# Loading the first 2 KiB of the first tile's runs from ScalarE's queue, beside the other 62 KiB from SP's

## Chip, cores, metric

One core of a Trainium2 chip. The metric is the device time of one execution in microseconds. A kernel's time is the median of its runs. A ratio is the mean time of one kernel's fast runs over that of the other's of the same rounds on the same chip, so it is not quite the ratio of the medians quoted; the brackets after it hold its 95% interval.

## The reference

```python
# x: (1024, 4096) float32, axis = -1
mean = np.mean(x, axis=axis, keepdims=True)
return ((x - mean) ** 2).astype(np.float32)
```

## The kernel before

Two tiles, each of 512 rows: 128 partitions with four rows of 4096 numbers each, so one contiguous run of 64 KiB for each partition. Both tiles stay in SBUF from the start; nothing waits for a buffer. The first load is cut: a small transfer of 2 KiB runs, then the other 62 KiB of each run.

```python
HEAD = 512
H = D * 9 // 16
...
for i in range(ntiles):                       # ntiles = 2
    x_tile = io.tile([P, Q * D], F32)         # Q = 4, D = 4096
    cuts = [0, HEAD, Q * D] if i == 0 else [0, Q * D]
    for lo, hi in zip(cuts, cuts[1:]):
        nc.sync.dma_start(out=x_tile[:, lo:hi], in_=x_t[i][:, lo:hi])
...
for i in range(ntiles):
    row = [tiles[i][:, q * D:(q + 1) * D] for q in range(Q)]
    m3 = mean_on_act(row[3])                  # ScalarE
    m0 = mean_on_dve(row[0])                  # VectorE: needs the small transfer too
    square_on_act(row[3], m3)
    m1 = mean_on_dve(row[1])
    square_on_act(row[0], m0)
    m2 = mean_on_dve(row[2])
    square_on_act(row[1], m1)
    square_on_act(row[2][:, :H], m2)
    back = row[2][:, H:]                      # VectorE ends the tile
    nc.vector.tensor_scalar_add(out=back, in0=back, scalar1=m2)
    nc.vector.tensor_mul(out=back, in0=back, in1=back)
    nc.sync.dma_start(out=out_t[i], in_=tiles[i])
```

## Time and profile before

| | before |
|---|---|
| time, median of the first 3 runs | 83.02 us (83.0 to 83.2) |
| span in the profile | 81.2 us |
| first byte moves / last byte has moved | 1.75 / 80.02 us |
| DMA engines busy | 96.2% of the span |
| VectorE starts on tile 0 / tile 0's store is issued | 22.47 / 39.42 us |
| that store's first packets start | 41.08 to 41.39 us |

The profile's lines stand in the prediction. Read them in this order: the busy shares (who could be the bound), the stretches (where bytes move and at what rate), the timeline (when a transfer is issued and when its reader starts). The trace also has a record of each DMA packet with its queue, size, start and duration. A packet here is one run of one partition, and each of the 16 DMA engines carries 8 of each transfer's 128. Numbers said to come "from the packet records" are counted there; the stretches show them only summed. The records do not name the engine: a packet is put on the engine whose packet before it ended when this one starts, and at a gap the ends and the starts are taken in the same order. The sums of packets and the mean gaps do not depend on that; the counts of engines do.

### The profile page before, as it was taken

To read this page: it belongs to the slowest core of one execution; us is meant where nothing else is said; L and a number is where in the kernel's file an instruction comes from. 1 tells how busy PE (TensorE), PEld (TensorE's weight loads), DVE (VectorE), ACT (ScalarE), POOL (GpSimd) and SP (SyncE) were. 2 spreads that over 40 slices of the span, in tenths; PEclk is the share of its full clock that TensorE was granted. 3 is DMA by queue.
4 is the path that set the end of the run, shared out by engine and by line. 5 is a ranking of instruction groups with operands and counts; after the bars stand their busy time and mean duration, and the time that the engine had idled before them with its cause. 6 is when DMAs were issued, how large, how long until landed. Compare 5 with 4: busy or idle time off the path is not lost.

```text
span 81.2 us, 83 instructions
## 1 busy us (share of the span) xinstructions
DVE 33.4 (41%) x16; ACT 34.7 (43%) x13; POOL 0.2 (0%) x4
## 2 busy tenths in 40 slices
DVE  0000000000099999999349999999800000000000
ACT  6000000000099999999249999999800000000000
POOL 0000000000000000000000000000000000000000
DMA  1999569999974999990999990999992899997490
GB/s 16 614 501 501 219 282 501 501 501 501 517 323 194 517 517 517 517 484 32 517 517 517 517 517 0 517 517 517 517 517 129 388 517 517 517 517 323 194 517 0
DMA packets 720, 33.55 MB, mean 413 GB/s; under 512 B 80, under 2 KB 80, under 8 KB 208
## 3 DMA queue, kind: packets, MB, share of 16 engines
q1 hardware_dynamic: 720, 33.55, 96.2%
HBM read 16.78 MB, written 16.78 MB: 413 GB/s over the span
## 4 chain that ended last, share of the span: by engine, by line
DMA 49%; DVE 21%; SPq 1%; issue 0%
DMA x_tile<-in_x_dram 49%; DVE neg_sum L66 16%; DVE x_tile L89 2%; DVE x_tile L88 1%; SPq L50 1%; DVE neg_mean L69 1%
## 5 line engine op out<-in xcount | busy, mean ns | idle before, releaser
L66 DVE TENSOR_REDUCE neg_sum<-x_tile 128x1 f32<-128x4096 f32 x6 | 26.5, 4413 | 24.9 <-DMA x_tile<-in_x_dram 24.9
L73 ACT ACTIVATE x_tile<-x_tile,neg_mean 128x4096 f32<-128x4096 f32 (+1 forms) x8 | 26.0, 3324 | 0.1
L58 ACT ACTIVATE copy<-x_tile 128x4096 f32<-128x4096 f32 x2 | 7.2, 3616 | 23.0 <-DMA x_tile<-in_x_dram 23.0
L89 DVE TENSOR_TENSOR x_tile<-x_tile 128x1792 f32<-128x1792 f32 x2 | 4.1, 2026 | 0.1
L88 DVE TENSOR_SCALAR x_tile<-x_tile,neg_mean 128x1792 f32<-128x1792 f32 x2 | 2.3, 1153 | 0.1
L58 ACT ACT_TABLE_LOAD x1 | 1.3, 1283 | 0.7 <-PEq L107 0.7
L69 DVE TENSOR_SCALAR neg_mean<-neg_sum 128x1 f32<-128x1 f32 x6 | 0.9, 154 | 0.2
L58 ACT ACTIVATION_READ_ACCUMULATOR copy<-x_tile 128x1 f32 x2 | 0.4, 186 | 0.0
L107 POOL MEMSET const-bfloat16-1.0<- 128x1 bf16 x1 | 0.1, 103 | 0.0
L107 POOL MEMSET const-uint8-127<- 128x1 uint8 x1 | 0.1, 103 | 0.0
L107 POOL MEMSET const-float32-1.0<- 128x1 f32 x1 | 0.1, 100 | 0.0
L107 POOL MEMSET const-float32-0.0<- 128x1 f32 x1 | 0.1, 99 | 0.2 <-issue 0.2
## 6 DMA issues: line engine op xcount, KB each, us to landing
x_tile<-in_x_dram SPq DMA_DIRECT2D x1, 7936.0 KB, 21.2
x_tile<-in_x_dram SPq DMA_DIRECT2D x1, 256.0 KB, 2.7
out_dram<-x_tile SPq DMA_DIRECT2D x2, 21.7
x_tile<-in_x_dram SPq DMA_DIRECT2D x1, 40.1
```

Of the source, the lines that this page charges most:

```text
L50: nc.sync.dma_start(out=x_tile[:, lo:hi], in_=x_t[i][:, lo:hi])
L58: nc.scalar.activation(out=copy, in_=row, func=ACT.Identity, scale=-inv_d, accum_out=neg_mean)
L66: inorder(nc.vector.reduce_sum(out=neg_sum, in_=row, axis=mybir.AxisListType.X, negate=True))
L69: inorder(nc.vector.tensor_scalar_mul(out=neg_mean, in0=neg_sum, scalar1=inv_d))
L73: inorder(nc.scalar.activation(out=part, in_=part, func=ACT.Square, bias=neg_mean, scale=1.0))
L88: nc.vector.tensor_scalar_add(out=back, in0=back, scalar1=m2)
L89: nc.vector.tensor_mul(out=back, in0=back, in1=back)
L107: nc = _bacc.Bacc("TRN2", target_bir_lowering=False, num_devices=1)
```

## The change

Its intent is to have the two issues for tile 0 made at the same moment by two engines, so that SP need not issue the small transfer first. The same bytes move in the same five transfers.

```diff
-        cuts = [0, HEAD, Q * D] if i == 0 else [0, Q * D]
-        for lo, hi in zip(cuts, cuts[1:]):
-            nc.sync.dma_start(out=x_tile[:, lo:hi], in_=x_t[i][:, lo:hi])
+        lo = 0
+        if i == 0:
+            lo = HEAD
+            nc.scalar.dma_start(out=x_tile[:, :lo], in_=x_t[i][:, :lo])
+        nc.sync.dma_start(out=x_tile[:, lo:], in_=x_t[i][:, lo:])
```

## The prediction

> **What bounds the kernel now.** I read the page's head and its DMA rows first, then the table of stretches, then the timeline, then the chain of waits. The page:
>
> ```profile
> span 81.2 us, 83 instructions
> DVE 33.4 (41%) x16; ACT 34.7 (43%) x13; POOL 0.2 (0%) x4
> ...
> q1 hardware_dynamic: 720, 33.55, 96.2%
> HBM read 16.78 MB, written 16.78 MB: 413 GB/s over the span
> ```
>
> VectorE and ScalarE are each busy for well under half of the span, while the 16 DMA engines are busy for 96.2% of it: 0.962 x 81.2 = 78.1 us. What is left is 3.1 us in all, and any gain must come out of that or out of the 78.1 us themselves. The busy time of each engine by stretch, with my cuts at the places where the trace's packet records change from one transfer to the next (columns: stretch, its length, busy time and instructions of VectorE, ScalarE and GpSimd, clock, DMA share, GB/s; a packet counts where it starts, so a share can pass 1):
>
> ```profile
> 0.00:1.75 1.75, 0.00 (x0) 1.02 (x1) 0.20 (x4) 1.00 0.00 0
> 1.75:2.65 0.90, 0.00 (x0) 0.26 (x1) 0.00 (x0) 1.00 0.82 189
> 2.65:22.05 19.40, 0.00 (x0) 0.00 (x0) 0.00 (x0) 1.00 1.12 478
> 22.05:41.40 19.35, 16.71 (x8) 16.72 (x6) 0.00 (x0) 1.00 1.00 434
> 41.40:60.70 19.30, 16.71 (x8) 16.72 (x6) 0.00 (x0) 1.00 0.99 431
> 60.70:80.05 19.35, 0.00 (x0) 0.00 (x0) 0.00 (x0) 1.00 0.88 383
> 80.05:81.20 1.15, 0.00 (x0) 0.00 (x0) 0.00 (x0) 1.00 0.00 0
> ```
>
> So there are five parts: 1.75 us before the first byte moves, 0.90 us for the 2 KiB runs (0.26 MB), four stretches of 19.3 to 19.4 us for the two loads and the two stores, and 1.15 us after the last byte. Compute (16.7 us for a tile on either engine) lies inside the second and third long stretch. The timeline shows when each transfer is issued and when compute starts:
>
> ```profile
> 0.73 1.28 ACT L58 ACT_TABLE_LOAD   x1 [0.73 <-PEq L107]
> 0.73 1.33 SPq L50 DMA_DIRECT2D x_tile<-in_x_dram  x3
> 22.39 3.62 ACT L58 ACTIVATE copy<-x_tile 128x4096 f32<-128x4096 f32 x1 [20.38 <-DMA x_tile<-in_x_dram]
> 22.47 4.42 DVE L66 TENSOR_REDUCE neg_sum<-x_tile 128x1 f32<-128x4096 f32 x1 [22.47 <-DMA x_tile<-in_x_dram]
> ...
> 39.42 19.62 SPq L90 DMA_DIRECT2D out_dram<-x_tile  x2
> ...
> 41.74 4.42 DVE L66 TENSOR_REDUCE neg_sum<-x_tile 128x1 f32<-128x4096 f32 x1 [2.39 <-DMA x_tile<-in_x_dram]
> ```
>
> The first store is issued at 39.42, before the second load has left the engines (the earliest engine ends it at 41.08 by the packet records). It is therefore already queued when an engine comes free, and the pipe never runs dry. The chain of waits names the load, then the second tile's VectorE work:
>
> ```profile
> 1.16 0.42 SPq L50
> 1.59 0.05 issue
> 1.64 40.08 DMA x_tile<-in_x_dram
> 41.72 0.02 issue
> 41.74 4.43 DVE neg_sum L66
> ```
>
> That chain stops at the last compute instruction (58.6 us) and does not see that the last store waits in the queue behind the first. It should not mislead: the bound is the stream of bytes from 1.75 to 80.05 us.
>
> **What the Trainium skill says.** First, "DMA: Bandwidth & Descriptors", section "Issuing engines are not separate DMA queues": transfers issued from SP and from ScalarE run on the same 16 engines and interleave, and a second issuer saves only the time of issuing. The trace before has a single queue, so it cannot show the interleaving; it does show what issuing costs, 1.33 us for three issues. Second, the same page, "Queues, rings and completion order": each engine goes round-robin between the queues that have work, a packet at a time. No run yet shows it. Third, the same page, "Latency and other measured facts": about 600 ns to the first byte for this kind of issue. Here the first packet starts 1.02 us after the issue starts (1.75 - 0.73), which is 0.64 us after its 0.38 us of issuing ends; that agrees. Fourth, "Perfetto Trace Analysis", "DMA Instruction — HWDGE (DVE, Sync)": the block that writes descriptors is shared between the issuers and locked for one at a time, so two issues at the same moment may still be served one after the other. Not shown yet either.
>
> **The change part by part.** The order of instructions against the kernel before shows just one move: the transfer of 128 runs of 2 KiB goes from first on SP's queue to first on ScalarE's, ahead of the table load. All waits, all compute and the other four transfers stay, and so does the number of transfers (five) and of packets (128 of 2 KiB, 128 of 62 KiB, 384 of 64 KiB).
>
> 1. Issuing. SP's 62 KiB runs were issued at 1.16 and are now at 0.73, which is 0.43 us earlier. What it is worth: the 2 KiB packets started at 1.75, and the first 62 KiB packet at 2.67. By the same 1.02 us its descriptors would have been there at 1.16 + 1.02 = 2.18, so it was waiting for an engine, not for its issue. The saved issue is thus hidden behind the small packets: 0 us. The other two transfers behind it were queued even longer: 0 us.
>
> 2. First byte. One of the two issues still starts at 0.73, so the first packet still starts near 1.75: 0 us. If the shared block makes one of them wait, the other feeds the engines meanwhile.
>
> 3. The bytes. By the packet records a small packet takes 84 ns at the median, a 62 KiB one 2342 and a 64 KiB one 2418. Each of the 16 engines carries 8 + 8 + 24 of them: 8 x 0.084 + 8 x 2.342 + 24 x 2.418 = 0.67 + 18.74 + 58.03 = 77.44 us. That is unchanged whatever the order. From the first packet's start to the last one's end is 78.27 us, so the stream loses 0.83 us altogether. That is the most that better filling could win.
>
> 4. The start-up loss. The small packets average 122 ns, not 84 (the first ones take 500 to 640): 8 x 0.038 = 0.30 us per engine. The 16 first 62 KiB packets average about 2.56 us, 0.22 above the median. With both queues ready, an engine has a large packet to fetch while the small one waits for memory, so part of these 0.52 us can go; but a first access must be waited for in any order. My estimate is a gain of 0.1 us, with 0.3 at most.
>
> 5. ScalarE. Its table load moves back by one issue, some 0.4 us, to about 1.13 to 2.41. Its first real work waits for data until 22.39, so this costs nothing.
>
> 6. When tile 0 lands. The small packets are needed by row 0, which VectorE reads first. In an alternation of one to one, the eighth small packet goes beside the eighth large one, so tile 0 lands at the same 22.4. There is room: VectorE's start at 22.47 leads to the store's issue at 39.42, with packets ready by the same 1.02 us at 40.44, and the first engine is free at 41.08. So 0.64 us of delay are hidden.
>
> Sum: 0 + 0 + 0 - 0.1 + 0 + 0 = -0.1 us on 83.02, so 82.9 us.
>
> **The rivals.** (a) The full start-up loss goes: the issue of the large runs is no longer 0.43 us late and the first 62 KiB packets run at their median. For it: the DMA share is only 0.82 in the stretch of the small packets. Against: the first large packet would have been ready at 2.18 and started at 2.67. It would give 83.02 - 0.5 = 82.5 us. (b) The shared queue costs something: switching rings at every packet for the 8 small packets of each engine, or a later first byte on a second queue. In the trace before, a 62 KiB packet follows another without a gap (starts are 2.34 us apart), and I have nothing to size a switch by; 8 switches of a small packet's time, 0.084 us, would make 0.7 us, so 83.7 us. (c) The small packets starve: if the engines drain SP's whole first load before ScalarE's queue, row 0 lands 0.67 us late, which is about the 0.64 us of room: 83.0 us still. If they came after SP's second load, VectorE would start some 19 us late and the pipe would run dry for most of that: near 100 us. The round-robin that the skill describes speaks against it, and so I give it 1 in 100. (d) Something outside the span: 83.02 - 81.2 = 1.8 us lie outside the profile, and a second queue in use could add to its set-up. Nothing in the trace bears on it; I allow a few tenths.
>
> **Range and chances.** The runs before spread from 83.0 to 83.2. Rival (a) marks the lower end, 82.5; (b) and (d), in weak forms, the upper, 83.4. A gain over 2% means under 81.36 us, so 1.66 us less. That is twice the 0.83 us that the stream loses, so I give it 1%. A loss over 2% means over 84.68 us; it needs rival (c) in its strong form, or a cost of a second queue that I don't know: 3%. Within 2%: 96%.
>
> **What would show it.** In the profile after: two queues in the DMA rows; the first packets still near 1.75 us; SP's 62 KiB runs issued at 0.73; ScalarE's table load at about 1.1; tile 0's first reduction near 22.4 and the first store's issue near 39.4; full stretches still at 431 to 435 GB/s; span 81.1. I am wrong if the first packet starts clearly later or earlier than 1.75, if VectorE's first wait ends more than 0.64 us later than 22.47 and a hole opens before the first store, or if the large packets beside the small ones take longer by more than the small ones' own time.

## The result and the profile after

The changed kernel takes 83.55 us (83.36 to 83.66, 6 runs) against 83.06 us (83.0 to 83.2, 6 runs): ratio 1.0052 [1.0035, 1.0069], 0.5% slower. It is within 2%, as forecast, but in the other direction and 0.15 us above the stated range.

The head of the page after, and its DMA issues (out<-in, engine, count, KB, us from issue to landing):

```profile
span 81.6 us, 83 instructions
...
q1 hardware_dynamic: 576, 33.29, 95.2%
q10 hardware_dynamic: 144, 0.26, 0.8%
...
x_tile<-in_x_dram SPq DMA_DIRECT2D x1, 7936.0 KB, 21.9
x_tile<-in_x_dram ACTq DMA_DIRECT2D x1, 256.0 KB, 22.1
```

There are two queues now. The small transfer, which landed 2.7 us after its issue before, now takes 22.1 us: it ends with the large one, not ahead of it. The same stretches as before:

```profile
0.00:1.75 1.75, 0.00 (x0) 0.60 (x1) 0.20 (x4) 1.00 0.11 36
1.75:2.65 0.90, 0.00 (x0) 0.68 (x1) 0.00 (x0) 1.00 3.20 1058
2.65:22.05 19.40, 0.00 (x0) 0.00 (x0) 0.00 (x0) 1.00 0.97 417
22.05:41.40 19.35, 16.71 (x8) 16.72 (x6) 0.00 (x0) 1.00 0.96 417
41.40:60.70 19.30, 16.71 (x8) 16.72 (x6) 0.00 (x0) 1.00 0.98 424
60.70:80.05 19.35, 0.00 (x0) 0.00 (x0) 0.00 (x0) 1.00 0.98 423
80.05:81.60 1.55, 0.00 (x0) 0.00 (x0) 0.00 (x0) 1.00 0.00 0
```

The 0.90 us in which before moved the small packets now hold the starts of large ones (a share of 3.20, since a packet counts where it starts). The later stretches shift accordingly; do not read their rates as a slower pipe without the packet records. The timeline:

```profile
0.73 0.86 SPq L52 DMA_DIRECT2D x_tile<-in_x_dram  x2
0.73 0.39 ACTq L51 DMA_DIRECT2D x_tile<-in_x_dram  x1
1.15 1.28 ACT L60 ACT_TABLE_LOAD   x1 [1.15 <-PEq L109]
22.70 3.62 ACT L60 ACTIVATE copy<-x_tile 128x4096 f32<-128x4096 f32 x1 [20.26 <-DMA x_tile<-in_x_dram]
22.90 4.42 DVE L68 TENSOR_REDUCE neg_sum<-x_tile 128x1 f32<-128x4096 f32 x1 [22.90 <-DMA x_tile<-in_x_dram]
...
39.85 19.48 SPq L92 DMA_DIRECT2D out_dram<-x_tile  x2
```

Both issues start at 0.73 and take the same 0.4 us. VectorE gets tile 0 at 22.90, 0.43 us later than before, and the store is issued 0.43 us later. What that does at the change from loading to storing shows in the stretches around it (same columns). Before, and then after:

```profile
39.40:41.05 1.65, 0.00 (x0) 0.00 (x0) 0.00 (x0) 1.00 0.00 0
41.05:41.40 0.35, 0.00 (x0) 0.00 (x0) 0.00 (x0) 1.00 6.93 2996
```

```profile
41.05:41.40 0.35, 0.00 (x0) 0.00 (x0) 0.00 (x0) 1.00 2.65 1124
41.40:41.95 0.55, 0.00 (x0) 0.00 (x0) 0.00 (x0) 1.00 2.80 1192
```

Before, all 16 engines start on the store between 41.05 and 41.40 (2996 GB/s x 0.35 us = 16 x 64 KiB). After, only six do (1124 x 0.35 us = 6 x 64 KiB), and ten come later. By the packet records every engine passes from load to store within 3 ns before, and stands still for 156 ns on average after.

The whole difference, from the packet records as a mean over the 16 engines:

| | before | after | difference |
|---|---|---|---|
| idle before the first packets | 0.21 | 0.11 | -0.09 |
| 8 small packets | 0.98 | 0.67 | -0.30 |
| 8 packets of 62 KiB | 19.00 | 19.48 | +0.48 |
| rest of the loading of tile 0 (small idle pieces) | 0.02 | 0.01 | -0.01 |
| gap between load and store | 0.00 | 0.16 | +0.15 |
| 24 packets of 64 KiB | 58.04 | 58.16 | +0.12 |
| idle at the end, until the last engine is done | 0.14 | 0.25 | +0.11 |
| sum of differences | | | +0.46 |

From the first packet's start to the last one's end it is 78.27 us before and 78.72 after, +0.44. The first four rows make too much of the start, since they add up packets that overlap by some ns (after the change a large packet starts 77 ns after the end of the one before it, with a small one of 84 ns between them). Tile 1's first packets start on average 20.16 us after the first packet of all before, and 20.22 us after it now. So the start of the stream costs 0.05 us more, the gap and the slower 64 KiB packets after it 0.27, and the engines' larger spread at the end 0.11.

Two details of the records matter. On all engines the order is large, small, large, small: SP's first packet starts at 1.75 us, and ScalarE's first small one only at 4.66, when that large one is done. And the first large packet of each engine takes 3.08 us on average, where later ones take 2.34.

### The profile page after: what moved, and what is told of

The parts are those of the page before. It is cut to its first block, busy times and chain, and to the rows that moved or that the text cites. A ratio compares the mean times of both kernels' runs of the same rounds, so it can differ in the third digit from the quotient of the medians.

```text
span 81.6 us, 83 instructions
## 1 busy us (share of the span) xinstructions
DVE 33.4 (41%) x16; ACT 34.7 (43%) x13; POOL 0.2 (0%) x4
## 4 chain that ended last, share of the span: by engine, by line
DMA 50%; DVE 21%; SPq 0%; issue 0%
DMA x_tile<-in_x_dram 50%; DVE neg_sum L68 16%; DVE x_tile L91 2%; DVE x_tile L90 1%; DVE neg_mean L71 1%; SPq L52 0%
## 6 DMA issues: line engine op xcount, KB each, us to landing
x_tile<-in_x_dram ACTq DMA_DIRECT2D x1, 256.0 KB, 22.1
```

## The experiments

The main theory, "late landing": the small packets, last in their alternation with the large ones, make tile 0 land late; so its store reaches the engines too late and a gap opens. The rivals: "cold start" (the first packet of an engine is slow, and dear if it has 62 KiB) and "two queues" (a second queue costs by itself).

**The changed kernel again.** 

> The changed kernel, unaltered, on the same chip as the others of this group. All theories: 1.005 of the kernel before, so 0.3 to 0.6 us slower. In the profile: first 62 KiB packets near 3.1 us (2.34 later), the large packet first and the small one second on every engine, VectorE's first wait ends near 22.9 us, and a gap of 0.1 to 0.2 us per engine between the second load and the first store.

Measured: 83.48 us against 83.07, 1.0046 [1.0032, 1.0060]. Large first again, first packets 3.04 us, VectorE's wait until 22.82, store issued at 39.78, gap 164 ns on all 16 engines. The loss repeats in rounds of its own.

**SP held back, so that the small packets go first.**

```diff
+            nc.gpsimd.memset(x_tile[:, lo:lo + 256], 0.0)   # SP's first load must wait for this
-        nc.sync.dma_start(out=x_tile[:, lo:], in_=x_t[i][:, lo:])
+        tc.keep_in_program_order(nc.sync.dma_start(out=x_tile[:, lo:], in_=x_t[i][:, lo:]))
```

> Two queues as in the changed kernel, but SP's first load waits for a GpSimd memset of 256 of its columns, so that ScalarE's small packets reach the engines first and SP's large ones some 0.3 to 0.5 us later. Late-landing theory (the small packets come last, tile 0 lands 0.4 us late and the first store reaches the engines after they are free): tile 0 is waited for until 22.4 to 22.5, no gap before the first store, and the time is that of before within 0.15 us (82.9 to 83.2). Cold-start theory (the first packets are 62 KiB long and take 3.1 us): the first large packet comes second and is cheap, so also the time of before. Two-queues theory (a second queue costs by itself): 83.4 to 83.7, as the changed kernel.

Measured: 83.12 us against 83.07, 1.0003 [0.9991, 1.0015]. Its timeline:

```profile
0.73 0.36 ACTq L51 DMA_DIRECT2D x_tile<-in_x_dram  x1
1.06 0.85 SPq L53 DMA_DIRECT2D x_tile<-in_x_dram  x2
...
22.59 3.62 ACT L61 ACTIVATE copy<-x_tile 128x4096 f32<-128x4096 f32 x1 [20.19 <-DMA x_tile<-in_x_dram]
22.70 4.42 DVE L69 TENSOR_REDUCE neg_sum<-x_tile 128x1 f32<-128x4096 f32 x1 [22.70 <-DMA x_tile<-in_x_dram]
...
39.66 19.60 SPq L93 DMA_DIRECT2D out_dram<-x_tile  x2
```

SP's load is issued 0.33 us later, and the loss is gone, to within 0.12 us (the upper end of the interval), with both queues in use. So a second queue costs next to nothing by itself. A cost of switching queues at every packet is not tested here, since no engine switches back and forth in this run. VectorE's wait ends later than I expected (22.70), and the gap is 15 ns on average. The records show that here no engine alternates: all eight small packets come first, and the first large one starts 6 ns after the small transfer's completion write.

**No small transfer at all.**

```diff
-        cuts = [0, HEAD, Q * D] if i == 0 else [0, Q * D]
+        cuts = [0, Q * D]
```

> One queue, and tile 0 loaded in one transfer of 64 KiB runs: the large packets go first, with no small ones. Cold-start theory: the first packets take about 3.1 us, the time is 83.4 to 83.6 as in the changed kernel. Late-landing theory: with one queue nothing lands after the large packets; tile 0 lands within 0.2 us of 22.4, the first store comes in time, and the time is within 0.2 us of before (82.9 to 83.3). Two-queues theory: as before, 83.0 to 83.1.

Measured: 83.20 us against 83.07, 1.0012 [1.0000, 1.0024]. The first packets take 3.05 us, as in the changed kernel, but only some 0.1 us is lost. So the dear first packet is real, but with the small gap below it is worth about a quarter of the loss (by the interval, at most about half); "cold start" falls as its main cause. The store came at 39.64, with a gap on 5 engines (39 ns on average).

**The store split, in both kernels.** Rows 0 and 1 of tile 0 are stored as soon as they are done.

```diff
         square_on_act(row[1], m1)
+        if i == 0:
+            nc.sync.dma_start(out=out_t[i][:, :2 * D], in_=tiles[i][:, :2 * D])
...
-        nc.sync.dma_start(out=out_t[i], in_=tiles[i])
+        lo = 2 * D if i == 0 else 0
+        nc.sync.dma_start(out=out_t[i][:, lo:], in_=tiles[i][:, lo:])
```

In the changed kernel: 

> The changed kernel, with tile 0's store in two halves: rows 0 and 1 as soon as they are done (near 34 us), rows 2 and 3 at the old time. So the engines have the first half's packets long before they need them. Late-landing theory: the gap before the first store goes and the time falls by 0.2 to 0.3 us, to 83.1 to 83.35, less than 0.2 us over before. Cold-start and two-queues theories: nothing of the loss goes, 83.4 to 83.7.

In the kernel before: 

> The kernel before with the store split as in the run that split the changed kernel's, whose loads' last 64 KiB packets took 3.4 us on average and whose time rose by 0.75 us. If a store queued early behind the loads slows their last packets whatever the loads' queues: the last 64 KiB load packets above 3.0 us here too, and 83.8 to 84.1. If that came from the two load queues: 83.0 to 83.2.

Measured: 84.23 us (1.0152 [1.0127, 1.0176]) and 84.35 us (1.0153 [1.0139, 1.0167]). Every theory missed the first. The gap did go (2 ns), but the last load packet of each engine took 3.37 us in place of 2.42, and 3.42 in the kernel before. The split has a cost of its own, the same in both, and cannot decide the question.

**Where that cost comes from.** One run queues the whole store early by leaving tile 0's row 2 undone (wrong); another stores two halves, but only when the tile is done.

```diff
# early
-        square_on_act(row[2][:, :H], m2)
-        back = row[2][:, H:]
-        ...                                # the two VectorE instructions on back
+        if i > 0:
+            ...                            # the same four lines
# halves
-        nc.sync.dma_start(out=out_t[i], in_=tiles[i])
+        for lo, hi in ([(2 * D, 4 * D), (0, 2 * D)] if i == 0 else [(0, 4 * D)]):
+            tc.keep_in_program_order(nc.sync.dma_start(out=out_t[i][:, lo:hi], in_=tiles[i][:, lo:hi]))
```

> The kernel before, with row 2 of tile 0 left undone (wrong result on purpose) so that the whole store is issued near 37 us, 2.4 us earlier, in one transfer of 64 KiB runs. If queueing a store early behind the loads is what made the loads' last packets slow in the split runs: those last packets take 3.0 us or more, and 83.8 to 84.3. If the smaller 32 KiB packets or the second issue did it: 2.43 us, no gap, 83.0 to 83.15.

> The kernel before with tile 0's store in two transfers of 32 KiB runs, rows 2 and 3 first and then rows 0 and 1, both issued only when the whole tile is done, near 39.4 and 39.8 us. If the early queueing was the cause in the split runs: last load packets 2.43 us, no gap, 83.1 to 83.25 (16 packets of 1.213 us in place of 8 of 2.418 cost 0.06 us). If the smaller packets were it: last load packets above 3.0 us, 83.8 to 84.3.

Measured: early 84.26 us, 1.0154 [1.0138, 1.0170]; halves 83.22 us, 1.0016 [1.0003, 1.0028]. In the early run the store is issued at 37.38, and in the stretches from the start of the last load packets on:

```profile
38.60:39.40 0.80, 0.00 (x0) 0.00 (x0) 0.00 (x0) 1.00 4.26 1311
39.40:41.70 2.30, 0.00 (x0) 0.00 (x0) 0.00 (x0) 1.00 0.00 0
41.70:42.70 1.00, 0.00 (x0) 0.00 (x0) 0.00 (x0) 1.00 2.43 1049
```

The 16 last load packets start in the first stretch, the 16 first store packets not before the third: the load packets take 3.41 us. So it is the early queueing, not the packet size or the second issue. A store can come too early as well as too late.

**The kernel before, its store made late.** An extra VectorE instruction in tile 0, its result unused, in five sizes N: 576 and 1216 columns first, then 32, 256 and 416 to find where the loss begins.

```diff
+        if i == 0:
+            junk = scratch.tile([P, N], F32)
+            inorder(nc.vector.tensor_scalar_add(out=junk, in0=row[2][:, H:H + N], scalar1=m2))
```

576 columns: 

> The kernel before, one queue, small packets first; only an extra VectorE instruction of about 0.42 us in tile 0 makes its store issue at about 39.85 us, as in the changed kernel. Late-landing theory: a gap of 0.1 to 0.2 us per engine opens before the first store, and the 64 KiB packets average 2423 ns as they did in the changed kernel, not 2418; the time goes up by 0.2 to 0.35 us, to 83.3 to 83.4. Theory that the loss is at the start of the stream (cold large packets, spread of the engines, a second queue): nothing happens, 83.0 to 83.15, as the 0.64 us of room worked out in the prediction would hide it.

1216 columns: 

> The same with about 0.80 us, store issue at about 40.2 us. Late-landing theory: beyond the room every further microsecond is lost in full: a gap of 0.5 us, time 83.65 to 83.8. With 0.64 us of room: a loss of about 0.2 us, 83.2 to 83.3.

32 columns: 

> The kernel before with an extra VectorE instruction of about 0.24 us in tile 0, by which its store is issued near 39.7 to 39.9 us. With room of 0.2 to 0.4 us, all or none on each engine (as a step of about 0.2 us that 0.52 and 0.85 us of delay paid alike, 0.27 and 0.33 us in time): the engines are mixed, mean gap 0.02 to 0.15 us, time 0.05 to 0.25 us over before. If the loss grew with the delay in proportion: 0.1 us over before with gaps of like size on all engines. If the room were 0.64 us: no gap, 83.05.

256 columns: 

> The kernel before with an extra VectorE instruction of about 0.35 us, store issue 39.8 to 39.95 us. If the point is the same for both kernels and lies below 39.78: gaps on all engines, mean 0.15 to 0.2 us, 83.3 to 83.4. If before's point is later than that of the changed kernel: gaps on few or no engines, 83.05 to 83.2.

416 columns: 

> The same with about 0.43 us, store issue 39.9 to 40.1 us. If before's point is later: mixed engines, mean gap 0.05 to 0.2 us, 83.15 to 83.4; if it is the same for both: all engines, 83.3 to 83.4.

Measured, with the one before for comparison; issue times from the timelines, the rest from the packet records, times against the same chip's before:

```
store issued  engines with a gap*  mean gap  first store packet  time and ratio
39.42 us       0 of 16               2 ns      2418 ns            (before)
39.69          0                     2         2418               83.10  1.0006 [0.9993, 1.0018]
39.94          7                    56         2428               83.20  1.0016 [0.9998, 1.0033]
40.08         16                   185         2456               83.30  1.0023 [1.0009, 1.0037]
40.19         16                   194         2457               83.39  1.0032 [1.0019, 1.0045]
40.41         16                   212         2460               83.45  1.0039 [1.0027, 1.0052]
* over 50 ns
```

The run with the store at 40.19, from its timeline and from a stretch that shows its gap:

```profile
40.19 19.05 SPq L93 DMA_DIRECT2D out_dram<-x_tile  x2
```

```profile
41.10:41.20 0.10, 0.00 (x0) 0.00 (x0) 0.00 (x0) 1.00 0.02 0
```

By the packet records four completion writes of 9 ns fall into this stretch, so loads have ended on some engines, and no store packet starts yet. With one queue and the old start of the stream, lateness alone brings the gap, and with it the slower packets: 2423 ns on average over all of the 64 KiB packets at 40.19, as in the changed kernel. The gap rises within some 0.4 us of delay and is then nearly flat: from 40.08 to 40.41 it grows by 27 ns for 330 ns of delay. My "0.5 us gap" for the largest dose was wrong. Nor is the gap only a wait for the store to arrive: at 40.41 every engine is on the store within 1.23 us of its issue, and in the changed kernel, with its mean gap of 156 ns, all but two engines end their load later than that (1.25 to 1.71 us after the issue).

**The changed kernel, its store made earlier.** VectorE leaves 256 columns of tile 0 unsquared (wrong); two further runs cut more, on both engines.

```diff
-        back = row[2][:, H:]
+        back = row[2][:, H + (256 if i == 0 else 0):]
# further cuts: 384 columns less for ScalarE and 640 for VectorE, then 768 and 896
-        square_on_act(row[2][:, :H], m2)
+        square_on_act(row[2][:, :H - (384 if i == 0 else 0)], m2)
```

> The changed kernel with 256 columns of tile 0 left unsquared by VectorE (wrong result on purpose), so that its store issues 0.3 us earlier, near 39.5 us, while the start of the stream stays as it was: two queues, large packet first, 3.0 us for the first ones, tile 0 waited for until 22.8 to 22.9. Late-landing theory: gap under 0.05 us, 64 KiB packets back at 2418 to 2419, time 83.15 to 83.3. Cold-start and two-queues theories: 83.4 to 83.6, as the changed kernel.

> The changed kernel with more of tile 0's row 2 left undone on both engines (wrong result on purpose), store issue near 39.15 us. If the changed loads only make the store late: it is earlier than before's 39.42, so no gap, and what is left is the start-up's share, 83.1 to 83.2. If a second queue drained late makes gaps of itself: some engines still have them, mean gap 0.02 us or more, 83.15 to 83.3.

> The same with the store near 38.8 us. No gap by either theory, unless the second queue makes gaps at any time. If a store queued too early slows the last load packets (3.4 us in the runs with the store near 37.4), their mean may begin to rise above 2.43 us: 83.05 to 83.5.

```
store issued  engines with a gap  mean gap  last load packet  time and ratio
38.83 us       0                    2 ns      2686 ns          83.42  1.0040 [1.0023, 1.0057]
38.99          0                    2         2559             83.29  1.0023 [1.0008, 1.0039]
39.44          6                   45         2418             83.18  1.0009 [0.9997, 1.0022]
39.78         16                  164         2418             83.48  1.0046  (the changed kernel again)
```

At 39.44 the start of the stream is as in the changed kernel (first packets 3.10 us, VectorE's wait until 22.83), yet most of the loss is gone. So most of the loss passes through the time of the store. But the changed kernel has gaps on 6 engines at 39.44, where the kernel before has none at 39.69: its loads also move the point up to which a store may come. And at 38.99 the store is already too early.

**A repair that keeps the result right: VectorE takes row 1 first.**

```diff
-        m0 = mean_on_dve(row[0])
+        f, g = (1, 0) if i == 0 else (0, 1)
+        mf = mean_on_dve(row[f])          # and so on, with f and g for 0 and 1
```

> The changed kernel, but VectorE sums row 1 of tile 0 first and row 0, which needs the small packets, second (right result). It then starts when ScalarE does, near 22.65 us, and the store is issued some 0.2 us earlier than in the changed kernel, near 39.6 us. Late-landing theory: the gap before the first store goes on most engines, mean 0.1 us or less, time 83.1 to 83.35. If a queue used by ScalarE or the 3 us first packets cost the rest: 83.4 to 83.6 still.

Measured: 83.40 us, 1.0039 [1.0027, 1.0052]. A miss. VectorE did start with ScalarE, but both at 22.84, and the store was issued at 39.79 with a gap of 156 ns. In the alternation the large transfer's own completion also comes behind the last small packet, so not waiting for the small one gains little, and tile 0 landed late in this run in any case.

**One queue, the large packets first.** Is it the second queue that moves the point, or that the large packets go first and the small ones last? Both runs use SP's queue only, and all of an engine's large packets of tile 0 come before its small ones (in the changed kernel they alternate); the second also leaves 256 columns unsquared (wrong).

```diff
-        for lo, hi in zip(cuts, cuts[1:]):
-            nc.sync.dma_start(out=x_tile[:, lo:hi], in_=x_t[i][:, lo:hi])
+        for lo, hi in reversed(list(zip(cuts, cuts[1:]))):
+            tc.keep_in_program_order(nc.sync.dma_start(out=x_tile[:, lo:hi], in_=x_t[i][:, lo:hi]))
```

> One queue, SP's, with the two loads of tile 0 in the other order: the 62 KiB runs first, the 2 KiB runs after them, then tile 1. Tile 0 lands last with its small packets, as in the changed kernel; store issue expected near 39.7 us. If the order is what moves the point: gaps on most engines, mean 0.1 to 0.16 us, 83.3 to 83.5. If the second queue does: gaps on few or none, 0.04 us or less, 83.1 to 83.2.

> The same with 256 columns of tile 0 left unsquared by VectorE (wrong result on purpose), store issue near 39.4 us, to be set beside the changed kernel with the same cut (39.44 us, gaps on 6 engines, mean 0.045 us, 83.18). If the order moves the point: some engines with gaps, mean 0.02 to 0.07 us. If the second queue does: none, and the time is that of the 64 KiB run without small packets, 83.1 to 83.2.

Measured: 83.52 us against 83.10, 1.0046 [1.0032, 1.0061], and 83.30 us, 1.0021 [1.0007, 1.0035]. The timeline of the first and its stretches around the change to storing:

```profile
22.87 4.42 DVE L66 TENSOR_REDUCE neg_sum<-x_tile 128x1 f32<-128x4096 f32 x1 [22.87 <-DMA x_tile<-in_x_dram]
...
39.83 19.62 SPq L90 DMA_DIRECT2D out_dram<-x_tile  x2
```

```profile
41.05:41.40 0.35, 0.00 (x0) 0.00 (x0) 0.00 (x0) 1.00 1.77 749
41.40:41.95 0.55, 0.00 (x0) 0.00 (x0) 0.00 (x0) 1.00 3.36 1430
```

Without a second queue all of the changed kernel is back: first packets 3.06 us, VectorE at 22.87, store at 39.83, four engines on the store by 41.40 (749 x 0.35 us = 4 x 64 KiB), a mean gap of 163 ns, and the same ratio of 1.0046. With the cut the store comes at 39.27, no engine has a gap, and half of the loss is gone. So the cause is the order of tile 0's packets: the large ones before the small ones. The queue is only how that order came about. It takes the small ones behind, too: the run without any lost 0.1 us. How much of the loss is the gap with what follows it is known only roughly: half of it went here and four fifths with the cut in the changed kernel (1.0021 and 1.0009 are left), and the two intervals overlap. The store at 39.27 does not say where the point lies between 39.27 and 39.83.

**What stays open.** Lateness alone is probably the smaller part: the changed kernel's store is 0.43 us late, and the kernel before, with its store 0.27 and 0.52 us late, lost 0.06% and 0.16% (at most 0.33% by the interval), against 0.5%. The rest is the start and end of the stream, and the earlier point. Open is why the large-first order moves the point from about 39.9 to about 39.4 us (with stores at 39.64 to 39.69 us the mean gap is 39 ns without small packets, 15 with SP held and 2 in the kernel before), and why 64 KiB packets stay some 5 ns slower after a gap. A guess, not shown: with large packets first the engines read further ahead of what they write, so they run out of load sooner. It fits that every later load packet of the changed kernel takes exactly 2342 or 2418 ns, with no scatter, and that the first store packet after a gap is 40 ns longer; no run tests it. No version tried beats the kernel before, and nothing in the runs points to one.

## Why the prediction was right or wrong

Right: the bound (five transfers of the same bytes, start to end), step 2 (first packet at 1.75 us both times), step 5 (table load at 1.15, free), and the class, within 2%. Step 1 had the right value for a wrong reason: the large packets were not "hidden behind the small packets" but went ahead of them, at 1.75, and even that gained nothing. Step 3's sum of packets at their median fits the kernel before, but not its "unchanged whatever the order": the 24 packets of 64 KiB took 58.16 us in place of 58.04, being slower after the gap. Its sign of "full stretches still at 431 to 435 GB/s" was badly chosen, since a packet counts where it starts; the stretches that it shows run from 383 to 478.

Wrong, step 6 first: it put tile 0's landing "at the same 22.4". From the packet records the last byte of tile 0 came 0.19 us later (22.24 for 22.05), and VectorE started 0.66 us after it in place of 0.42, perhaps because both completions now come at the end (not tested). Together that is the 0.43 us seen. The step then had "0.64 us of delay" hidden, worked out by taking the store's packets as ready 1.02 us after issue, and the engine as needing them only when free. The late-store runs show otherwise: in the kernel before the room over 39.42 is at least 0.27 us (no gap at 39.69) and used up on 7 engines at 0.52, and in the changed kernel the point is earlier still. The time to arrive cannot be the whole of it (1.23 us at most, and 14 of the changed kernel's engines came free later than that after the issue); what failed is above all the assumption that an engine needs the store only when it is free. What follows is a gap of 0.16 to 0.21 us and slower packets behind it, 0.27 us together in the profiled pair.

Step 4 was wrong in sign. It expected 0.1 us back from the start-up loss, by fetching a large packet while a small one waits. The small packets did fall from 0.98 to 0.67 us per engine, but the first large ones went up from 2.55 to 3.08 us, and the start came out 0.05 us dearer, with another 0.11 us at the end from the larger spread of the engines. The run without a small transfer puts the price of a large first packet at about 0.1 us. That is what the cut in the kernel before was good for. (Its "500 to 640" for the first small packets holds for five of them; most of the others that are first to start take less.)

Of the rivals, (c) had the right link, small packets landing last and row 0 late, but dismissed its weak form as hidden by that same 0.64 us, and expected it only if ScalarE's queue were drained after SP's. Plain alternation with the large packet first was enough. Rival (b) had two forms. A cost of a second queue in use is refuted to within 0.12 us by the run with SP held back. A cost of switching at every packet shows nowhere in the records of the changed kernel (small packets at 84 ns, large ones 77 ns apart with a small one between), and the whole loss came back on one queue, where nothing switches. The range was too narrow by 0.15 us because its upper end came from (b) and (d), while the loss came from a sum that step 6 had set to zero.

## What to carry to other kernels

The transfer on another queue was not faster here (22.1 us to landing for 2.7), and it gave up its place in the order: before moving a small load that a reader waits for, ask which of the two will reach the engines first. In this kernel, which fills its DMA engines from start to end, a store was best queued neither when the loads had nearly run out (0.2 us lost per engine) nor well before (1 us lost), so moving a landing by 0.4 us cost time that no busy share shows. Work out such room from a run with an added delay, not from a difference of two times in one profile.

## What the Trainium skill lacked or had wrong

- "DMA: Bandwidth & Descriptors", "Queues, rings and completion order": the round-robin by packets is seen in the changed kernel, one run of a partition at a time, eight times large-small on all 16 engines. But with SP's issue 0.33 us later all eight small packets of each engine went ahead of the first large one. By the 1.02 us from an issue to its first packet SP's packets were due at 2.08 us (an estimate), and they started only at 2.72 us and later, when the small ones were done; the page does not tell from when on a queue counts as having work. It also lacks what the order between two issuers can cost: VectorE got tile 0 0.43 us later.
- "Perfetto Trace Analysis", "DMA Instruction — HWDGE (DVE, Sync)": a block locked for one issuer at a time would let one issue wait. Both were issued at 0.73 us and took 0.38 and 0.39 us, no longer than alone (0.38); no waiting shows in the issue times.
- No page that I read has the cost of passing from load to store on one engine: 2 ns with the store queued in time, 0.16 to 0.21 us with it late, and a last load packet of 3.4 us in place of 2.42 with it queued 1.2 us or more before that packet starts.
- No page that I read has the price of a large first packet: 2.9 to 3.1 us for the first 62 or 64 KiB of each engine in the runs that begin with them, against 2.34 or 2.42 later.
